# A depthwise convolution moved to tap matrices on TensorE, in a hybrid encoder layer

## The chip, the cores and the metric

The kernel runs on one core of a Trainium2 chip. The metric is the device time of one execution in microseconds (us). Names used: TensorE or PE (matrix products; "PEld" is its weight load), VectorE or DVE, ScalarE or ACT, GpSimd or POOL, SyncE or SP (it issues all the DMAs of this kernel). One execution is also recorded by the hardware profiler; durations of single instructions come from that one.

## What is computed

One encoder layer for 1024 tokens of width 1024, in float32. The part that matters here, shortened:

```python
p = h @ w_in + b_in                       # 3072 columns: conv value, conv gate, q, f, v, g (512 each)
u = p_value * sigmoid(p_gate)
y = depthwise_causal_conv(u, w_dw) + b_dw # 31 taps, 512 channels
cv = silu(group_norm(y) * gain + bias)    # 8 groups of 64 channels, per token
hg = hgrn2(q, f, v, g)                    # 4 heads of 128; gated linear recurrence over the tokens
y = concat(cv, hg) @ w_out                # then RMS norm, gate, residual
y2 = relu(h2 @ w_up) ** 2 @ w_down        # channel mixing, D_FF = 4096; then norm, gate, residual
```

## The kernel before

All engines' instructions are put in order when the kernel is built. `Weave` (line 168) is a small planner: it keeps a clock for each engine, charges each instruction an assumed cost (lines 251 to 254), and lets generators ("streams") run when their due time has come or their condition holds. The order found this way is the order in which each engine executes; on the chip an engine waits where an operand is late. SBUF is a pool of 53 slots of 128 x 1024 float32 (`Slots`); rings of slots hold loads (`stage`) and weights (`wring`).

Products of the main path are made of three matmuls of float32r (high part times high, high times low, low times high; `mm_k`, `mm_half`, `mm_step`), so every operand is split first into two slots (`split`: a copy by ACT, a subtraction by DVE or POOL). Matmuls of plain float32 operands run as two passes, and the trace counts two instructions for each of them.

The stages follow one another on PE:

- Start (to 76.7 us in the profiled execution): x is normalised and transposed, the modulation is computed, and three column blocks of `w_in` (`FIRST`) are multiplied as h arrives.
- Mixer (to 403.2 us): `mixer` (line 1076) goes through the column blocks of `w_in` in `ORDER`, 48 matmuls of 512 columns each (tiles `pj`). Weights are the stationary side, so a result has 128 channels as rows and all tokens as columns. v is the exception: `v_mm` (line 851) takes tokens as the stationary side, 256 columns at a time.
- Projection out (to 528.7 us): `out_mm` makes six token tiles from the blocks `EARLY` first, adds the blocks `LATE` later (tiles `pout`), and `out_tile` normalises, adds the residual and prepares h2.
- Up and down (to 1152.7 us): the feed-forward part in a two-level scheme of block products (tiles `pup`, `al`, `be`). The change does not touch its code.

Beside the projections, four blocks of the convolution run as streams. `conv_gate` and `conv_val` make u with channels as rows. `conv_near` (line 667) applies 20 taps by DVE, one scalar_tensor_tensor over up to 1024 tokens for each, into the PSUM tile `cacc`. `conv_far` (line 640) applies the other 11 taps in halves, with products by ACT or POOL and sums by POOL. `conv_norm` (line 685) transposes the result to tokens as rows (tile `cpt`), normalises in halves, and transposes back (tile `cpb`).

The four heads of the recurrence run as streams too. `head_att` (line 778) builds one score tile `att` for one head at a time. Blocks of h = 1, 2, 4, ... 64 tokens are joined level by level: PE computes the products of a level (tile `pl`), DVE multiplies the query, key and decay arrays for the next level, and for the levels in `MASKED` (1, 2, 4, 8) DVE copies the results under a mask. For h = 2, 4, 8 a level is one matmul with all 128 rows of a token tile as stationary side and 64 moving columns, for each of 8 token tiles; for h = 16, 32, 64 there is one matmul for each block of h. `head_state`, `head_out` and `put_mix` finish the head (tiles `tn`, `pS`, `po`, `pot`).

`mods_mid` loads further modulation weights (32 loads of `wada_n` in the whole kernel) and reduces them by DVE at a low rank. SP issues every load and store in one order.

## Time and profile before

| | us |
|---|---|
| median of 3 runs | 1161.85 (1156.34 to 1162.74) |
| profiled execution | 1161.52 |
| its span, first to last instruction | 1159.7 |
| mean granted TensorE clock in it | 0.971 of full |
| DMA traffic | 183.96 MB, 159 GB/s on average |

The table is read from the top: the profiled execution lies within the runs, so its durations can be set against the median. The granted clock is the share of full speed that the throttle allowed PE, averaged over the span.

### The profile page before, as it was taken

What the parts mean: (1) busy time and instruction counts of PE and PEld (TensorE: products, weight loads), DVE (VectorE), ACT (ScalarE), POOL (GpSimd) and SP (SyncE); (2) the same over time, 40 slices, a digit from 0 to 9 for tenths busy, and PEclk for the clock granted to TensorE, in tenths of its full rate; (3) what the DMA queues carried; (4) which work ended last, traced back from release to release, by engine and by line L of the source; (5) the groups of instructions that cost most, each with busy time, mean ns of one, the idle gap of its engine ahead of it and who ended that gap; (6) DMA issues with size and microseconds to landing.
All of it is one profiled execution on the core that took longest, in us unless ns stands there. A gap on an engine that the chain in (4) does not pass through costs nothing.

```text
span 1159.7 us, 14360 instructions
## 1 busy us (share of the span) xinstructions
PE 1090.5 (94%) x5606; PEld 909.5 (78%) x5606; DVE 845.0 (73%) x798; ACT 491.7 (42%) x691; POOL 479.6 (41%) x348
## 2 busy tenths in 40 slices
PE   3899879899998999978999999999999999999996
PEld 3787769787797788857888888888888888888885
DVE  5968988899999986464754986432356969996942
ACT  5643133323433353557544233566543434444520
POOL 6527778756688682484200232223400001304301
PEclk6899889989999999989999999999999999999999
DMA  9423213322311020355467774423666866674801
GB/s 371 165 65 109 74 54 110 127 80 85 92 37 37 26 85 1 117 210 200 145 256 276 293 263 164 135 76 133 220 254 228 319 225 231 246 262 158 323 22 73
DMA packets 50899, 183.96 MB, mean 159 GB/s; under 512 B 5648, under 2 KB 5904, under 8 KB 50832
## 3 DMA queue, kind: packets, MB, share of 16 engines
q1 hardware_dynamic: 50832, 183.05, 44.5%
q8 instruction: 44, 0.72, 0.3%
q14 instruction: 23, 0.19, 0.0%
HBM read 149.47 MB, written 33.55 MB: 158 GB/s over the span
## 4 chain that ended last, share of the span: by engine, by line
PE 54%; DVE 1%; POOL 0%; ACT 0%; DMA 0%; issue 0%; DVEq 0%; POOLq 0%; ACTq 0%
PE pup L1731 26%; PE al L1731 15%; PE be L1731 11%; PE pout L1731 1%; PE pt L1735 1%; DVE s L194 1%; POOL s L194 0%; ACT junk L194 0%; DMA x2d<-s 0%; PE pg L1731 0%; DVEq L1834 0%; POOLq L1834 0%; POOL last_ss L194 0%; POOL fr L194 0%; ACTq L1834 0%
## 5 line engine op out<-in xcount | busy, mean ns | idle before, releaser
L194 POOL TENSOR_TENSOR s<-s,s 128x1024 fp32r<-128x1024 f32 (+9 forms) x164 | 303.7, 1866 | 479.5 <-ACT s L194 443.6
L194 DVE TENSOR_TENSOR s<-s,s 128x1024 fp32r<-128x1024 f32 (+3 forms) x333 | 413.9, 1282 | 80.5 <-ACT s L194 56.1
L194 ACT ACTIVATE s<-s 128x1024 fp32r<-128x1024 f32 (+4 forms) x317 | 298.4, 972 | 298.9 <-DVE s L194 192.1
L1731 PE MATMUL pup<-s,s 128*128 128x512 f32 x1344 | 309.1, 391 | 0.0
L1731 PEld LDWEIGHTS pup<-s,s 128*128 128x128 f32 x1344 | 252.4, 188 | 52.1
L1731 PE MATMUL pj<-s,s 128*128 128x512 f32 (+1 forms) x1200 | 252.1, 366 | 0.0
L1731 PEld LDWEIGHTS pj<-s,s 128*128 128x128 f32 x1200 | 202.4, 193 | 33.0 <-ACT s L194 0.3
L1731 PE MATMUL al<-s,s 128*128 128x512 f32 x768 | 175.6, 390 | 3.1 <-DVE s L194 3.1
L1731 PEld LDWEIGHTS al<-s,s 128*128 128x128 f32 x768 | 143.9, 188 | 34.2 <-DVE s L194 4.3
L1731 PE MATMUL be<-s,s 128*128 128x512 f32 x576 | 131.0, 389 | 0.0
L1731 PEld LDWEIGHTS be<-s,s 128*128 128x128 f32 x576 | 108.1, 188 | 22.5
L1731 PE MATMUL pout<-s,s 128*128 128x512 f32 x384 | 96.4, 401 | 8.4 <-DVE s L194 8.3
L194 DVE SCALAR_TENSOR_TENSOR cacc<-s,vec,cacc 128x1023 f32<-128x1023 f32 (+18 forms) x76 | 96.9, 1275 | 1.1
L1731 PEld LDWEIGHTS pout<-s,s 128*128 128x128 f32 x384 | 71.1, 191 | 23.8 <-DVE s L194 9.2
L194 DVE SCALAR_TENSOR_TENSOR s<-s,c_act,s 128x1024 f32<-128x1024 f32 (+1 forms) x48 | 68.6, 1430 | 19.4 <-DMA s<-in_wada_n 18.0
L194 DVE SCALAR_TENSOR_TENSOR s<-pup,s 128x1024 f32<-128x1024 f32 x16 | 19.6, 1225 | 53.3 <-PE pup L1731 50.4
L194 DVE TENSOR_TENSOR s<-pup,s 128x1024 f32<-128x1024 f32 x24 | 29.3, 1222 | 40.0 <-PE pup L1731 40.0
L194 ACT ACTIVATE s<-s,vec 128x512 f32<-128x512 f32 (+5 forms) x40 | 28.3, 710 | 58.4 <-POOL s L194 58.3
L1731 PEld LDWEIGHTS pl<-s,s 128*16 128x16 f32 (+3 forms) x640 | 34.0, 137 | 21.9 <-issue 15.9
L1731 PE MATMUL pl<-s,s 128*16 128x16 f32 (+3 forms) x640 | 35.9, 222 | 14.8 <-DVE s L194 12.7
L1731 PE MATMUL pf<-s,s 128*128 128x512 f32 x144 | 41.3, 429 | 5.2 <-DVE s L194 3.7
L194 POOL TENSOR_SCALAR s<-s,vec 128x512 f32<-128x512 f32 (+6 forms) x44 | 45.3, 1031 | 0.0
(119 smaller groups left out, 757.1 us busy)
## 6 DMA issues: line engine op xcount, KB each, us to landing
s<-in_wdn SPq DMA_DIRECT2D x72, 512.0 KB, 5.2
s<-in_wup SPq DMA_DIRECT2D x56, 512.0 KB, 5.6
s<-in_wada_n SPq DMA_DIRECT2D x32, 512.0 KB, 3.5
s<-in_win SPq DMA_DIRECT2D x17, 512.0 KB, 3.6
s<-in_x SPq DMA_DIRECT2D x16, 512.0 KB, 6.4
s<-in_wada_t SPq DMA_DIRECT2D x16, 512.0 KB, 9.8
u<-s SPq DMA_DIRECT2D x16, 512.0 KB, 2.9
s<-u SPq DMA_DIRECT2D x16, 512.0 KB, 4.5
```

What stands on the lines that cost most here:

```text
L194: return op(*a, **k)
L1731: return self.te.matmul(out, lhsT=lhsT, rhs=rhs, **k)
L1735: return self.te.transpose(out, in_, identity)
```

## The change

The convolution becomes a product with matrices of taps. Value, gate and v are now computed with tokens as the stationary side (`t_mm`, four steps of 256 tokens each; the kinds `'U'`, `'G'` and `'V'` in `ORDER`), with their 512 columns as the moving side. u is written to a DRAM tensor `udram` in blocks of 32 tokens, one 512-byte piece for each token and quarter of the channels. `conv_input` loads it back in two passes of 256 channels: each partition takes one contiguous piece of 16 KiB, 63 token rows (31 of the block before and 32 of the block itself, a row of ones standing for the bias) twice over the two halves of the partitions. `conv_mm` multiplies each channel's 64 x 32 matrix of taps (loaded from the new input `toep`) with the 32 blocks as columns: 512 matmuls in plain float32. Their results come out with the tokens of a block as rows; ACT evacuates them, the normalisation runs over full tiles, and one transpose back remains (32 instead of 64 transposes for the convolution).

The levels h = 2, 4, 8 of the recurrence are issued as four matmuls of 32 stationary columns and 16 moving columns each, with results in four groups of 32 rows of PSUM; the masked copies become four of 32 rows. There are two score tiles, so a head may start while the one before it is unfinished. The planner's costs, the order of the column blocks, the early and late blocks, and ring sizes change with it. Four of the 53 slots become one wide tile while the convolution runs.

The core of the diff (imports of host arrays, slot bookkeeping and unchanged steps are left out):

```diff
-FIRST = (4, 0, 12)
-ORDER = (5, 8, 13, 9, 1, 6, 16, 2, 7, 14, 21, 10, 20, 3, 15, 18, 23, 11, 22)
+FIRST = (12, 8, 13)
+ORDER = (9, 20, 'V0', 'V1', 'V2', 'V3', 'G0', 'G1', 'G2', 'G3', 21, 'U0', 'U1', 'U2', 'U3', 14, 10, 22, 15, 11, 23)
-EARLY, LATE = (0, 4, 2, 5, 1, 6), (3, 7)
+EARLY, LATE = (4, 5, 0, 1, 2, 3), (6, 7)
-R0, STAGE, WRING = 12, 3, 6
+R0, STAGE, WRING, WRING1 = 12, 3, 12, 4
...
-    V = wv.engine(nc.vector, "V", lambda op, n: (0.13 if "scalar" in op else 0.07) + n / 960)
-    A = wv.engine(nc.scalar, "A", lambda op, n: 0.17 + n / 1190)
-    G = wv.engine(nc.gpsimd, "G", lambda op, n: 0.1 + n / (1000 if op == "tensor_scalar" else 460))
+    V = wv.engine(nc.vector, "V", lambda op, n: 0.16 + n / 930)
+    A = wv.engine(nc.scalar, "A", lambda op, n: 0.22 + n / 1190)
+    G = wv.engine(nc.gpsimd, "G", lambda op, n: 0.55 + n / (1350 if op == "tensor_scalar" else 520))
...
-    def conv_gate(j, ps):
-        yield room(1)
-        u = convs[j]["u"] = new()
-        A.activation(u.f, ps, AF.Sigmoid, bias=bcol(4 + j))
...
-    def conv_far(j):
...
-    def conv_near(j):
...
+    udram = dram.tile([4, CB, NB + 1, P], F32, name="udram")
+    crow_s = new()
+    S.dma_start(crow_s.f, crow.broadcast_to([P, 1024]))
+    sig = [None] * 4
+    ys = [None] * 4
+    u_rows = [0]
+
+    def t_gate(s, ps):
+        sig[s] = slots.new_last()
+        V.tensor_tensor(sig[s].f.rearrange("p (a c) -> p a c", c=512), ps.rearrange("p (a c) -> p a c", c=512),
+                        crow_s.f[:, None, H0].broadcast_to([P, 2, 512]), ALU.add)
+        A.activation(sig[s].f, sig[s].f, AF.Sigmoid)
+        yield
+
+    def t_val(s, ps):
+        yield room(1)
+        u = new()
+        V.tensor_tensor(u.f.rearrange("p (a c) -> p a c", c=512), ps.rearrange("p (a c) -> p a c", c=512),
+                        crow_s.f[:, None, H1].broadcast_to([P, 2, 512]), ALU.add)
+        mm.done(ps, "V")
+        G.tensor_tensor(u.f, u.f, sig[s].f, ALU.mult)
+        yield after("G")
+        for a in range(2):
+            for r in range(4):
+                b0 = 1 + 8 * s + 4 * a
+                nc.sync.dma_start(udram[r, :, b0:b0 + 4, :].rearrange("i q c -> q i c"),
+                                  u.f[:, (4 * a + r) * P:(4 * a + r + 1) * P])
+        wv.spend("S", 6.0)
+        u.release()
+        sig[s].release()
+        u_rows[0] += 1
+        if u_rows[0] == 4:
+            crow_s.release()
+            wv.add(conv_input(), RCONV)
+
+    def conv_input():
+        yield slots.gone
+        w = slots.wide().rearrange("p (b c) -> p b c", c=P)
+        for r in range(2):
+            S.dma_start(w[64 * r:64 * r + 1, 0, :], ones[0:1, :])
+            nc.sync.dma_start(w[64 * r:64 * r + 1, 1:, :], ones[1:CB, :])
+        for p in range(2):
+            yield room(4)
+            toeps = [new() for _ in range(4)]
+            for c in range(4):
+                S.dma_start(toeps[c].f, toep[p, c])
+            for r in range(2):
+                nc.sync.dma_start(w[64 * r + 1:64 * r + CB, :, :], udram[2 * p + r, 1:CB, 0:NB, :])
+                nc.sync.dma_start(w[64 * r + CB:64 * r + 64, :, :], udram[2 * p + r, :, 1:NB + 1, :])
+                wv.spend("S", 3.0)
+            yield wv.t["S"] + DLAT
+            yield from conv_mm(p, w, toeps)
+        slots.end_wide()
+
+    def conv_mm(p, w, toeps):
+
+        for q in range(2):
+            yield acc.free
+            ps = acc.take(ps_acc("cv"))
+            for i in range(16):
+                m = 16 * q + i
+                for c in range(4):
+                    for r in range(2):
+                        rows = slice(64 * r, 64 * r + 64)
+                        TE.matmul(ps[CB * c:CB * c + CB, 512 * r + CB * i:512 * r + CB * i + CB],
+                                  lhsT=toeps[c].f[rows, CB * m:CB * m + CB], rhs=w[rows, :, CB * c + m],
+                                  start=True, stop=True, us=0.03)
+            if q:
+                free(toeps)
+            wv.add(conv_evac(p, q, ps), 0)
+            yield
+
+    acc = Banks(wv, 1)
+
+    def conv_evac(p, q, ps):
+        pv = ps.rearrange("p (r i b) -> p r i b", r=2, i=16)
+        for s in range(4):
+            if ys[s] is None:
+                yield room(1)
+                ys[s] = new()
+            yv = ys[s].f.rearrange("t (b p r q i) -> t p q r i b", p=2, r=2, q=2, i=16)
+            for r in range(2):
+                A.activation(yv[:, p, q, r], pv[:, r, :, 8 * s:8 * s + 8], AF.Copy)
+        acc.done(ps, "A")
+        yield after("A")
+        if p and q:
+            for s in range(4):
+                wv.add(conv_norm(s), RNORM)
+
+    def conv_norm(s):
+
+        y = ys[s]
+        yield after("A")
+        yv = y.f.rearrange("p (a c) -> p a c", c=64)
+        mu = tiny("gmu", 16)
+        V.reduce_sum(mu, yv, axis=AX.X)
+        V.tensor_tensor(yv, yv, mu[:, :, None].broadcast_to([P, 16, 64]), ALU.subtract)
+        yield room(2)
+        sz, z = new(), new()
+        A.activation(sz.f, y.f, AF.Square)
+        var = tiny("gvar", 16)
+        V.reduce_sum(var, sz.f.rearrange("p (a c) -> p a c", c=64), axis=AX.X)
+        r = rstd_of(var, 16, 1.0 / 64, 1e-5, "gr")
+        V.tensor_tensor(yv, yv, r[:, :, None].broadcast_to([P, 16, 64]), ALU.mult)
+        for h in range(2):
+            yield aux_free
+            pb = ps1("cpb")
+            for b in range(4):
+                TE.transpose(pb[:, b * P:(b + 1) * P], y.f[:, (4 * h + b) * P:(4 * h + b + 1) * P], ident)
+            yield after("PE", 0.2)
+            pv = pb.rearrange("p (b c i) -> p c b i", c=4, i=CB)
+            zv = z.f[:, HALF[h]].rearrange("p (c b i) -> p c b i", c=4, i=CB)
+            for c in range(4):
+                A.activation(zv[:, c], pv[:, c], AF.Identity, bias=col(V_GNB + c), scale=col(V_GNG + c))
+            done1(pb, "A")
...
-    att_s = new()
-    att = att_s.f.rearrange("p (n t) -> p n t", t=P)
-    G.memset(att_s.f, 0.0)
+    att_s = [new(), new()]
+    atts = [t.f.rearrange("p (n t) -> p n t", t=P) for t in att_s]
+    for t in att_s:
+        G.memset(t.f, 0.0)
+    S.dma_start(udram[:, :, 0, :].rearrange("r i c -> (r i) c"), att_s[1].f[:, 0:P])
...
-        yield lambda: att_turn[0] == j
+        yield lambda: att_turn[0] >= j - 1
+        att = atts[j % 2]
...
-                    TE.matmul(pl[:, n * 64:(n + 1) * 64], lhsT=K[:, n * P:(n + 1) * P],
-                              rhs=Qn[:, n, :, 1, :], start=True, stop=True)
+                    for g in range(4):
+                        o = g * 32
+                        TE.matmul(pl[o:o + 32, n * 16:(n + 1) * 16], lhsT=K[:, n * P + o:n * P + o + 32],
+                                  rhs=Qn[:, n, g * nb // 4:(g + 1) * nb // 4, 1, :], start=True, stop=True, us=0.015)
...
-                V.copy_predicated(av[:, :, :, 1, :],
-                                  mk[:, None, :, :].broadcast_to([P, NT, nb, h]), plv)
+                if h == 1:
+                    V.copy_predicated(av[:, :, :, 1, :],
+                                      mk[:, None, :, :].broadcast_to([P, NT, nb, h]), plv)
+                else:
+                    plg = pl[:, 0:P].rearrange("p (n b i) -> p n b i", n=NT, i=h)
+                    for g in range(4):
+                        o, bs = g * 32, slice(g * nb // 4, (g + 1) * nb // 4)
+                        V.copy_predicated(av[o:o + 32, :, bs, 1, :],
+                                          mk[o:o + 32, None, bs, :].broadcast_to([32, NT, nb // 4, h]),
+                                          plg[o:o + 32])
...
-    def v_mm(j0):
...
+    def t_mm(kind, s):
+
+        if s == 0:
+            yield loads[0].has(4)
+            tws[:] = [loads[0].get() for _ in range(4)]
+        yield mm.free
+        ps = ps2("pt" + kind)
+        for k in range(KT):
+            w = tws[k // 2]
+            for q in range(2):
+                tsl = slice((2 * s % 4 + q) * P, (2 * s % 4 + q + 1) * P)
+                mm_half(TE, ps[:, HALF[q]], [t[:, tsl] for t in h_halves(k)[s // 2]],
+                        [t[:, HALF[k % 2]] for t in w], k == 0, k == KT - 1)
+            if s == 3 and k % 2:
+                if kind == [j for j in ORDER if isinstance(j, str) and j[0] in TGROUPS][-1][0]:
+                    wring.n = WRING1
+                loads[0].used()
+            yield
+        wv.add(dict(G=t_gate, U=t_val, V=v_evac)[kind](s, ps), 0)
+
+    tws = []
+
+    def v_evac(s, ps):
+        pv = ps.rearrange("p (n c) -> p n c", n=2)
+        if s == 0:
+            yield room(4)
+            for hd in heads:
+                hd["v"] = new()
+        yield lambda: "v" in heads[3]
+        for j, hd in enumerate(heads):
+            V.tensor_tensor(hd["v"].f[:, 256 * s:256 * s + 256].rearrange("p (n c) -> p n c", n=2),
+                            pv[:, :, j * P:(j + 1) * P],
+                            vbias[:, None, j * P:(j + 1) * P].broadcast_to([P, 2, P]), ALU.add)
+            hd["vh", s] = True
```

More of the change, by code (lines that the diff above doesn't have):

```diff
@@ L375, in x_load @@
     def x_load(n):
[L376 removed]
+        xn[n] = slots.new_last() if n < NWIDE else new()
         S.dma_start(xn[n].f, x[n * P:(n + 1) * P, :])
@@ L571, in rest @@
         for j in ORDER:
-            srcs += [winv[(j - 16) // 2, i] for i in range(2)] if 16 <= j < 20 else [win[j]]
+            if isinstance(j, int):
+                srcs.append(win[j])
+            elif j[1] == "0" and j[0] in TGROUPS:
+                srcs += [wint[TGROUPS.index(j[0]), i] for i in range(4)]
         loads.append(Loads(srcs, wring))
@@ L614, in put_mix @@
         yield from split(full, hi.r[:, sl], lo.r[:, sl])
-        marks.t["mix", kt, half] = wv.now
-    def tap(j, s):
-        return col(V_WDW + j * TAPS + PADW - s)
-    convs = [dict() for _ in range(4)]
+        for n in range(4):
+            marks.t["mix", kt, half * 4 + n] = wv.now
     heads = [dict() for _ in range(4)]
-    def conv_gate(j, ps):
-        yield room(1)
-        u = convs[j]["u"] = new()
-        A.activation(u.f, ps, AF.Sigmoid, bias=bcol(4 + j))
-        mm.done(ps, "A")
-        yield
@@ L665, in block_kernel @@
-    near_turn = [0]
-    def conv_near(j):
-        c = convs[j]
-        uf = c["u"].f
-        yield lambda: near_turn[0] == j
-        acc = ps_acc("cacc")
-        for s in range(0, TAPS - POOL_TAPS):
-            yield idle("V", NEAR)
-            if s == 0:
-                V.tensor_scalar(acc, uf, tap(j, 0), col(V_BDW + j), ALU.mult, ALU.add)
-            else:
-                V.scalar_tensor_tensor(acc[:, s:], uf[:, 0:T - s], tap(j, s), acc[:, s:], ALU.mult, ALU.add)
-        yield lambda: "far" in c
-        V.tensor_tensor(c["pacc"].f, acc, c["pacc"].f, ALU.add)
-        c["u"].release()
-        near_turn[0] += 1
-        for half in range(2):
-            wv.add(conv_norm(j, half), RNORM)
@@ L685, in conv_norm @@
-    def conv_norm(j, half):
-        y = convs[j]["pacc"]
-        yield after("V")
-        yield aux_free
-        pt = ps1("cpt")
-        for q in range(4):
-            n = half * 4 + q
-            TE.transpose(pt[:, q * P:(q + 1) * P], y.f[:, n * P:(n + 1) * P], ident)
-        yield after("PE", 0.2)
-        pv = pt.rearrange("p (a c) -> p a c", c=64)
-        mu = tiny("gmu", 8)
-        V.reduce_sum(mu, pv, axis=AX.X)
-        yield room(1)
-        scr = new()
-        yc, sq = scr.f[:, H0], scr.f[:, H1]
-        ycv = yc.rearrange("p (a c) -> p a c", c=64)
-        var = tiny("gvar", 8)
+        A.activation(sig[s].f, sig[s].f, AF.Sigmoid)
@@ L712, in conv_norm @@
         yield after("V")
-        yield aux_free
-        pb = ps1("cpb")
-        for q in range(4):
-            TE.transpose(pb[:, q * P:(q + 1) * P], yc[:, q * P:(q + 1) * P], ident)
-        yield after("PE", 0.2)
-        z, sz = yc, sq
-        A.activation(z, pb, AF.Identity, bias=col(V_GNB + j), scale=col(V_GNG + j))
-        done1(pb, "A")
-        A.activation(sz, z, AF.Sigmoid)
+        for h in range(2):
[9 more added lines that the diff above has]
+            done1(pb, "A")
@@ L722, in conv_norm @@
+        y.release()
+        A.activation(sz.f, z.f, AF.Sigmoid)
         yield after("A")
+        V.tensor_tensor(z.f, z.f, sz.f, ALU.mult)
+        sz.release()
+        yield after("V", 0)
         yield room(2)
-        yield from put_mix(j, half, lambda o: V.tensor_tensor(o, z, sz, ALU.mult))
-        scr.release()
-        if half:
-            y.release()
+        hi, lo = mix[s % 2, s // 2] = pair()
+        yield from split(z.f, hi.r, lo.r)
+        z.release()
+        for n in 2 * s, 2 * s + 1:
+            for k in range(4):
+                marks.t["mix", k, n] = wv.now
@@ L885, in head_state @@
     def head_state(j):
         hd = heads[j]
-        yield lambda: ("vh", 0) in hd and ("vh", 1) in hd
+        yield lambda: all(("vh", s) in hd for s in range(4))
         v, f = hd["v"].f, hd["f"].f
@@ L1008, in gate_rows @@
         acc.release()
-        grow[i] = new()
-        g = grow[i].f
+        gs = new()
+        g = gs.f
         yield ring.room()
@@ L1055, in mods_mid @@
     def mods_mid():
-        yield from gate_rows(0, stage)
         yield from ffn_cols(0, stage)
         yield from ffn_cols(1, stage)
+        yield from gate_rows(0, stage)
     for j, ps in zip(FIRST, pfirst):
@@ L1065, in load_wo @@
     def load_wo(k):
-        yield lambda: len(slots.free) >= WOSPARE + 2 and bool(stage.room()())
+        yield lambda: slots.left() >= WOSPARE + 2 and bool(stage.room()())
         hi, lo = pair()
@@ L1305, in stream @@
                 need = len(srcs) + extra
-                yield lambda: self.out < AHEAD and len(slots.free) >= need + RES
+                yield lambda: self.out < AHEAD and slots.left() >= need + RES
                 raws = []
```

205 lines of the change are left out of this document (96 added, 109 removed).

## Prediction

> **What bounds the kernel now.** I read the busy times first, then the slices by stage, then the chain that ended last, then the waits of the matmul engine in the one stage that is not full.
>
> ```profile
> span 1159.7 us, 14360 instructions
> PE 1090.5 (94%) x5606; PEld 909.5 (78%) x5606; DVE 845.0 (73%) x798; ACT 491.7 (42%) x691; POOL 479.6 (41%) x348
> PE 54%; DVE 1%; POOL 0%; ACT 0%; DMA 0%; issue 0%; DVEq 0%; POOLq 0%; ACTq 0%
> 0.00:23.50 23.50, 7.64 (x34) 6.86 (x34) 11.75 (x28) 14.12 (x28) 15.11 (x26) 0.67 0.93 362
> 23.50:76.70 53.20, 47.82 (x229) 38.27 (x229) 39.97 (x62) 29.41 (x54) 21.73 (x23) 0.89 0.45 167
> 76.70:403.20 326.50, 301.27 (x1925) 258.35 (x1925) 301.39 (x293) 105.70 (x188) 241.49 (x169) 0.96 0.23 73
> 403.20:528.70 125.50, 116.38 (x694) 96.44 (x692) 80.81 (x95) 66.09 (x132) 74.10 (x63) 0.97 0.33 116
> 528.70:844.30 315.60, 311.77 (x1387) 257.82 (x1386) 178.75 (x136) 153.74 (x156) 75.35 (x34) 0.99 0.54 192
> 844.30:1152.70 308.40, 305.27 (x1345) 251.78 (x1343) 230.18 (x184) 121.99 (x134) 50.91 (x32) 1.00 0.60 216
> ```
>
> The stage rows give start:end, length, busy time of PE, PEld, DVE, ACT and POOL, the granted clock, the DMA share and GB/s. The two feed-forward stages (528.7 on) are filled by PE at a clock of 0.99 to 1.00; the chain, followed back from the end, is PE through all of them. Nothing of the change lies there. The mixer (76.7 to 403.2) is different: PE and VectorE are both 92% busy (301.27 and 301.39 of 326.5 us) at a clock of 0.96. The projection out (to 528.7) has PE 93% busy at 0.97. I call these two the region: 452.0 us. Its PE waits:
>
> ```profile
> PE pl L1731 <- DVE s L194: 16.9, 12, 3.5
> PE pout L1731 <- DVE s L194: 8.3, 1, 8.3
> PE po L1731 <- DVE s L194: 2.9, 2, 2.7
> PE pot L1735 <- ACT s L194: 2.5, 2, 1.9
> PE pl L1731 <- DVE gsf L194: 2.0, 1, 2.0
> PE pg L1731 <- DVE s L194: 1.3, 1, 1.3
> ...
> PE pt L1735 <- POOL s L194: 3.8, 1, 3.8
> ```
>
> The last row lies behind 528.7 us and is used further down. The others are 33.9 us, 31.4 of them ended by VectorE. The lost clock adds 0.04 x 326.5 + 0.03 x 125.5 = 16.9 us (an estimate from the stage rows). So the region holds about 51 us in which PE waits or runs slowly, and the order of the instructions is fixed beforehand: PE cannot take later work while a level waits.
>
> **The change part by part, on PE.** Rates first: a 512-column matmul starts every 43.52/192 = 0.227 us; a 256-column one every (347.15 - 338.43)/72 = 0.121 us.
>
> ```profile
> 1018.75 43.52 PE al L1731 x192
> 338.43 8.88 PE L1731 MATMUL pj<-s,s 128*128 128x256 f32 x72
> 347.15 0.62 PE L1731 MATMUL pd<-s,ones_r 128*128 128x512 f32 x2
> ```
>
> *Projections.* Gate, value and v move from weights-stationary to tokens-stationary. Gate and value keep 2 x 192 matmuls of 512 columns; v goes from 384 of 256 to 192 of 512: 46.5 - 43.5 = **-3.0 us**.
>
> *Recurrence levels 2, 4, 8.* Before, each is 8 matmuls with 128 weight columns; the trace has two passes per float32 matmul:
>
> ```profile
> 125.48 1.89 PE L1731 MATMUL pl<-s,s 128*128 128x64 f32 x16
> 127.18 4.37 PE L1731 MATMUL pj<-s,s 128*128 128x512 f32 x18
> 147.57 0.71 PE L1731 MATMUL pl<-s,s 128*16 128x16 f32 x64 [2.87 <-DVE s L194]
> 148.20 5.77 PE L1731 MATMUL pj<-s,s 128*128 128x512 f32 x18
> 154.15 0.70 PE L1731 MATMUL pl<-s,s 128*32 128x32 f32 x32 [0.18 <-DVE s L194]
> 154.78 4.39 PE L1731 MATMUL pj<-s,s 128*128 128x512 f32 x18
> ```
>
> A level of the old form takes 127.18 - 125.48 = 1.70 us. The new form is 32 matmuls of 32 weight columns and 16 moving ones. The trace has 32 matmuls of 16 and 16 in 0.63 us, and 16 of 32 and 32 in 0.63 us (0.039 each). So the new level costs 0.63 to 32 x 0.039 = 1.26; I take 0.63, whose count and moving size are the same. 4 heads x 3 levels x (1.70 - 0.63) = **-12.8 us** (-5.3 at the other end).
>
> *Convolution.* 512 float32 matmuls of 64 rows, 32 weight columns and 32 moving columns (2 passes x 2 halves x 16 channels x 4 x 2), with moving elements 128 apart, in eight separate corners of the array. No row has that form. From below, 0.63/32 = 0.020 each, 10 us; from above 1.70/8 = 0.21 each, 109 us, if nothing overlaps. I take the nearest row, 32 and 32 columns: 512 x 0.039 = **+20.2 us**.
>
> The first of these rows bears on a rule of the Trainium skill: TensorE: Matmul & The Clock Gate, section "Wait — 56ns, not 53.3ns?", says that matmuls start no closer than about 25 ns however small they are. The trace does not agree: 64 passes in 0.63 us are one per 10 ns. By the page 1024 passes of the convolution would be 25.6 us and a level 1.6, an estimate, and the sum below 17 us higher.
>
> *Transposes.* 32 of the convolution's 64 go:
>
> ```profile
> 170.96 0.60 PE L1735 MATMUL cpt<-msk,s 128*128 128x128 f32 x4
> 171.31 0.96 PE L1731 MATMUL pj<-s,s 128*128 128x256 f32 x6
> ```
>
> 8 x 0.35 = **-2.8 us**.
>
> **VectorE and the waits.** What leaves VectorE:
>
> ```profile
> L194 DVE SCALAR_TENSOR_TENSOR cacc<-s,vec,cacc 128x1023 f32<-128x1023 f32 (+18 forms) x76 | 96.9, 1275 | 1.1
> L194 DVE TENSOR_SCALAR cacc<-s,vec 128x1024 f32<-128x1024 f32 x4 | 5.4, 1340 | 0.1
> L194 DVE TENSOR_TENSOR s<-cacc,s 128x1024 f32<-128x1024 f32 x4 | 4.9, 1224 | 3.6 <-POOL s L194 3.5
> L194 DVE TENSOR_TENSOR s<-pout,s 128x1024 f32<-128x1024 f32 x7 | 8.4, 1218 | 1.9 <-PE pout L1731 1.9
> L194 DVE SCALAR_TENSOR_TENSOR s<-s,s,pS 128x128 f32<-128x128 f32 x24 | 8.3, 347 | 0.7
> L194 DVE COPY_PREDICATED s<-msk,pl 128x512 f32<-128x512 uint32 x16 | 16.1, 1008 | 0.0
> ```
>
> The taps are 96.9 + 5.4 + 4.9 = 107.2 us. The new work, by the full-width row (1.22 us) and the 128-column one (0.35): 8 bias adds and some 24 full-width steps of the norm and splits, 39 us, of which about that much stood there before in halves; 16 v evacuations of 256 columns, about 0.5 each, 8 us; and 12 masked copies become 48 of 128 columns, 12 x (1.4 - 1.0) = 5 us. So about 95 of 382 us leave, and the share falls from 85% of the region to some 69% of a shorter one. POOL loses the far taps as well; ACT loses its tap products and gets 32 small evacuations (0.28 us for 128 columns), far below its 172 of 452 us.
>
> What do the waits become? At least nothing changes (0), at most all 51 us go. The nearest row is the up stage, VectorE 57% busy, with clock 0.99 and 3.8 us of PE idle: 2% of its length, 10 us in 452. The head chains (levels one after another) remain here, so I leave 15 us: **-36 us**. What is late next is the chain of levels itself and then the convolution's norm.
>
> **What is costed at nothing, and its cover.** The DRAM round trip: 2.1 MB out, 4.2 MB in, 4.2 MB of tap matrices, some 32 GB/s in a stage that moves 73. The 32 stores wait on SP for POOL's product; behind them stand weight loads, hence PE, and the cover is two projection blocks (48 x 0.227 = 10.9 us each). The convolution's matmuls are a new wait on PE for the block loads; behind them stand the projections of heads 2 and 3 and all levels still open, and ACT and VectorE wait for those. The norm must end before the second part of the early output tiles; its cover is 6 tiles x 6 x 6 x 0.227 = 49 us of out-projection. Without it some 20 us of norm would show. Head work starts earlier, and two score tiles let two heads overlap; that is in the 36.
>
> **Sum**, against the profiled execution's own 1161.5 us (span 1159.7 and 1.8 around it; the median of the runs is 1161.85): 1161.5 - 3.0 - 12.8 - 2.8 + 20.2 - 36 = **1127 us**. Its own range: waits -51 to -15, convolution 10 to 30 us: 1102 to 1158.
>
> **Rivals.**
>
> (1) *The block loads are late; slower than before.* Each of the two passes loads, for both row halves, 31 partitions of 16 KiB (508 kB) and 32 more. The first stage row shows what one of 16 DMA engines moves: 362/(16 x 0.93) = 24.3 kB/us. If a load of 31 pieces cannot be shared out, it takes 20.9 us, and two queue on the same engine: 41.8 us a pass. The plan in the code allows 3.0 us a load pair and 2.0 after it. Counting its 6.0 for the stores and 5.8 for the tap matrices, PE reaches the matmuls some 30 us early in each pass (stores 7 and loads 44 against 20; then 44 against 14) and waits 60 us in all. Other engines catch up meanwhile (-10), the cold clock costs 3: 1127 + 53 = **1180**, from 1145 to 1195. It decides from 17 us of wait a pass: there the gain of 34 is gone. For: 31 pieces cannot be shared evenly among 16 engines, and the plan prices this load like any other. Against: every load in the trace spreads evenly, 512 KB in 3.6 us, so the trace shows no such case.
>
> ```profile
> s<-in_win SPq DMA_DIRECT2D x17, 512.0 KB, 3.6
> ```
>
> The Trainium skill speaks for this rival: DMA: Bandwidth & Descriptors, section "Why a DMA increments its semaphore by 16 and not by 1", lets a transfer use the largest number of engines up to 16 that divides the slowest dimension of both sides, which for 31 is one. No run here shows it yet.
>
> (2) *The waits stay.* If they come from the levels' order and not from VectorE's load, only some 8 us go: **1155**. For: the level waits are short (16.9 us in 12). Against: no wait of PE before 403 us is ended by anything but a VectorE that is 92% busy, save 2.5 us.
>
> (3) *The small matmuls do not overlap*: 109 us for the convolution, **1216**. Against: 32 matmuls in 0.63 us.
>
> **How the numbers follow.** Forecast 0.45, rival 1 0.35, rival 2 0.13, rival 3 0.07. A change within 0.5% (5.8 us) is what a measurement of this kernel cannot tell from none. Faster: 0.45 + 0.2 x 0.35 + 0.5 x 0.13 = 0.58. Within: 0.15 x 0.35 + 0.4 x 0.13 = 0.11. Slower: the rest, 0.31. The range runs from the forecast's low end, 1102, through rival 1 to 1190; outside are rival 3 and the tails, under 0.2.
>
> **What would show it.** Each step has its place in the changed profile: a level of 2, 4 or 8 at 0.63 us; the convolution at 20 us of PE between first and last; VectorE below 75% in the mixer; PE waits on VectorE under 15 us. Rival 1 would show as one or two PE waits of about 30 us ended by the block loads, with DMA nearly idle; rival 2 as level waits of today's size. The forecast fails if the round trip is late or if the mixer's own chain, heads 2 and 3 at its end, becomes longer than the work that covers it.

## The result, and the profile after

The changed kernel takes 1236.71 us (median of 4 runs, 1235.92 to 1241.32) against 1160.07 us for the one before in the same job: ratio 1.0671, 95% interval 1.0629 to 1.0714. It is slower by about 77 us, on the side of rival 1 and beyond the upper end of the range.

The profiled execution (1237.09 us) by stage, as in the prediction: start:end, length, busy time of PE, PEld, DVE, ACT and POOL, granted clock, DMA share, GB/s. The second fence is the share line of its chain of waits.

```profile
span 1234.9 us, 17034 instructions
23.50:79.10 55.60, 49.09 (x228) 38.68 (x228) 39.28 (x60) 29.33 (x54) 24.35 (x25) 0.89 0.44 162
79.10:309.60 230.50, 223.79 (x1607) 183.80 (x1606) 119.34 (x170) 48.50 (x100) 41.19 (x22) 0.99 0.36 107
309.60:433.90 124.30, 40.84 (x1302) 33.35 (x1301) 19.98 (x28) 13.11 (x39) 3.76 (x2) 0.64 0.21 67
433.90:467.50 33.60, 29.65 (x223) 23.37 (x221) 31.65 (x40) 12.52 (x17) 15.26 (x7) 0.91 0.16 49
467.50:606.80 139.30, 123.16 (x865) 100.14 (x864) 88.48 (x106) 75.82 (x159) 64.82 (x51) 0.91 0.32 105
606.80:919.50 312.70, 310.61 (x1390) 256.77 (x1388) 178.75 (x135) 155.37 (x158) 78.81 (x36) 1.00 0.56 195
919.50:1227.90 308.40, 305.27 (x1344) 251.90 (x1343) 228.95 (x183) 121.81 (x134) 53.44 (x33) 1.00 0.62 216
```

```profile
PE 72%; DMA 9%; DVE 9%; issue 4%; POOL 2%; ACT 2%; another core or an unknown queue 2%; SPq 0%; DVEq 0%; POOLq 0%; ACTq 0%
```

Up and down are as they were (621.1 us against 624.0). The region, 452.0 us before, is now 79.1 to 606.8: 527.7 us, +75.7. The four rows of the region have PE busy for 223.79 + 40.84 + 29.65 + 123.16 = 417.4 us; before it was 301.27 + 116.38 = 417.7. **So PE's busy time came out the same; the whole loss is PE standing still**, 110.3 us where it was 34.3. The chain of waits has 9% DMA in it, where it had 0%. The second row (79.1 to 309.6 us) has PE 97% busy at a clock of 0.99, where the mixer before had 92% at 0.96; that fits VectorE's relief, but other things changed with it. The third row says where the time went: 124.3 us with PE 33% busy, the other engines 3 to 16%, and a DMA share of 0.21. PE's waits in the region (engine, tile, line, what ended them: total, times, longest), and the convolution's matmuls on PE in order of time:

```profile
PE cv L1833 <- DMA wide<-udram: 53.3, 3, 19.9
PE cv L1833 <- issue: 28.3, 6, 19.0
PE pout L1833 <- POOL s L234: 5.8, 1, 5.8
PE pout L1833 <- DVE s L234: 4.1, 1, 4.1
PE pl L1833 <- DVE s L234: 3.6, 4, 1.5
PE cpb L1837 <- ACT s L234: 3.5, 1, 3.5
```

```profile
328.61 0.28 PE L1833 MATMUL cv<-wide,s 64*32 64x32 f32 x2 [18.98 <-issue]
348.77 2.81 PE L1833 MATMUL cv<-wide,s 64*32 64x32 f32 x247 [19.87 <-DMA wide<-udram]
353.30 0.33 PE L1833 MATMUL cv<-wide,s 64*32 64x32 f32 x7 [1.73 <-issue]
...
394.21 0.28 PE L1833 MATMUL cv<-wide,s 64*32 64x32 f32 x2 [13.56 <-DMA wide<-udram]
414.33 2.69 PE L1833 MATMUL cv<-wide,s 64*32 64x32 f32 x236 [19.83 <-DMA wide<-udram]
```

Each pass stops twice: before its first matmul, and again after one matmul (two passes of the array, "x2"), which needs only the upper half of the partitions. Four waits, 72.2 us. The 18.98 us put down to "issue" are the same kind: the chain of waits has the loads there, issued on SP at these times:

```profile
296.57 0.35 SPq L722 DMA_DIRECT2D wide<-udram  x1
297.33 0.27 SPq L722 DMA_DIRECT2D wide<-udram  x1
364.98 0.24 SPq L722 DMA_DIRECT2D wide<-udram  x1
365.69 0.23 SPq L722 DMA_DIRECT2D wide<-udram  x1
```

```profile
296.57 30.62 DMA wide<-udram
365.97 48.22 DMA wide<-udram
```

The two loads of 31 rows (line 722) were issued 0.76 us apart, and the second released PE 348.77 - 328.61 = 20.2 us after the first, in the second pass 20.1 us. 508 kB in about 20 us is 25 kB/us, what one of the 16 DMA engines moved in the first stage row (24.3). While PE waits, the DMA share is 0.11, and through 19.8 us of the wait for the second load it is 0.06, about one engine of 16, at 26 GB/s:

```profile
309.60:353.60 44.00, 3.42 (x258) 3.12 (x257) 2.52 (x2) 1.06 (x1) 3.76 (x2) 0.53 0.11 39
328.90:348.70 19.80, 0.00 (x0) 0.00 (x0) 0.00 (x0) 0.00 (x0) 0.00 (x0) 0.50 0.06 26
```

The first load of each pair took longer: it landed 30.6 us after its issue in the first pass and released PE 29.2 us after it in the second. Tap matrices and loads of 32 rows were under way beside it; what share of the longer time is theirs isn't shown.

### The profile page after: what moved, and what is told of

It reads as the page before. It is cut to its first block, busy times and chain, and to the rows that moved or that the text cites. A ratio compares the mean times of both kernels' runs of the same rounds, so it can differ in the third digit from the quotient of the medians.

```text
span 1234.9 us, 17034 instructions
## 1 busy us (share of the span) xinstructions
PE 1091.9 (88%) x6988; PEld 896.1 (73%) x6988; DVE 721.3 (58%) x751; ACT 471.8 (38%) x687; POOL 298.1 (24%) x200
## 4 chain that ended last, share of the span: by engine, by line
PE 72%; DMA 9%; DVE 9%; issue 4%; POOL 2%; ACT 2%; another core or an unknown queue 2%; SPq 0%; DVEq 0%; POOLq 0%; ACTq 0%
PE pup L1833 24%; PE al L1833 14%; PE be L1833 11%; DVE s L234 7%; DMA wide<-udram 6%; PE pout L1833 6%; PE ptG L1833 3%; PE pj L1833 3%; PE ptV L1833 3%; POOL s L234 2%; PE ptU L1833 1%; PE pf L1833 1%; ACT s L234 1%; PE pl L1833 1%
## 5 line engine op out<-in xcount | busy, mean ns | idle before, releaser
L234 DVE TENSOR_TENSOR s<-s,s 128x1024 fp32r<-128x1024 f32 (+4 forms) x342 | 407.3, 1229 | 123.7 <-ACT s L234 73.9
L234 ACT ACTIVATE s<-s 128x1024 fp32r<-128x1024 f32 (+2 forms) x317 | 304.5, 993 | 330.0 <-DVE s L234 195.8
L234 POOL TENSOR_TENSOR s<-s,s 128x1024 fp32r<-128x1024 f32 (+3 forms) x87 | 198.5, 2290 | 595.0 <-ACT s L234 519.1
L234 DVE SCALAR_TENSOR_TENSOR s<-s,c_act,s 128x1024 f32<-128x1024 f32 (+1 forms) x48 | 58.0, 1208 | 105.2 <-DMA s<-in_wada_n 103.9
L1833 PE MATMUL pj<-s,s 128*128 128x512 f32 x432 | 109.3, 412 | 0.0
L1833 PEld LDWEIGHTS pj<-s,s 128*128 128x128 f32 x432 | 85.7, 200 | 19.0 <-ACT s L234 0.3
L1833 PE MATMUL cv<-wide,s 64*32 64x32 f32 x1024 | 13.1, 245 | 81.6 <-DMA wide<-udram 53.3
L1833 PEld LDWEIGHTS cv<-wide,s 64*32 64x32 f32 x1024 | 11.7, 124 | 84.2 <-issue 84.2
L1833 PE MATMUL ptV<-s,s 128*128 128x512 f32 x192 | 48.0, 398 | 0.0
L1833 PE MATMUL ptG<-s,s 128*128 128x512 f32 x192 | 45.8, 394 | 0.0
```

Source lines behind the costliest of these rows:

```text
L234: return op(*a, **k)
L1833: return self.te.matmul(out, lhsT=lhsT, rhs=rhs, **k)
```

## The experiments

Theory A is rival 1: each load of 31 rows runs on a single DMA engine, so the convolution's operands are late. Its rivals are that something else in those loads is slow (their 16 KiB pieces), that only the place of the matmuls in PE's order is wrong, or that the rest of the forecast failed too. Ratios are to the kernel before in the same job (1159 to 1160 us).

**1. The loads.** The first run issues the 31 rows as 16 and 15; the second keeps 31 rows and divides the pieces.

```diff
# e1
-nc.sync.dma_start(w[64 * r + 1:64 * r + CB, :, :], udram[2 * p + r, 1:CB, 0:NB, :])
+nc.sync.dma_start(w[64 * r + 1:64 * r + 17, :, :], udram[2 * p + r, 1:17, 0:NB, :])
+nc.sync.dma_start(w[64 * r + 17:64 * r + CB, :, :], udram[2 * p + r, 17:CB, 0:NB, :])
# e2
+for b in range(0, NB, 8):
+    nc.sync.dma_start(w[64 * r + 1:64 * r + CB, b:b + 8, :], udram[2 * p + r, 1:CB, b:b + 8, :])
```

> The changed kernel; each load of 31 rows is issued as one of 16 rows and one of 15, same order of everything else. Theory A (a load whose row count shares no divisor with 16 engines runs on one engine, 20 us each, two in a row per pass): the PE waits ended by the block loads fall from about 82 us to under 15, and the time from 1237 to 1140-1165. Theory B (pieces of 16 KiB, or 32 partitions written at once, are slow whatever the row count): no change, 1230-1245.

> The changed kernel; each load of 31 rows is issued as four loads of 31 rows with pieces of 4 KiB. Theory A: each still runs on one engine, so the waits stay at about 82 us and the time at 1230-1245. Theory B: the pieces are now those of the other loads of the kernel, so the waits fall under 30 us and the time under 1190.

With 16 and 15 rows: 1182.43 us, ratio 1.0206 (1.0177 to 1.0235). With 31 rows in pieces of 4 KiB: 1239.19 us, 1.0704 (1.0668 to 1.0741). The waits of the convolution's matmuls in e1, then the second waits of both passes in e2:

```profile
PE cv L1834 <- DMA wide<-udram: 11.7, 3, 6.2
PE cv L1834 <- issue: 11.3, 6, 3.1
```

```profile
353.65 2.79 PE L1834 MATMUL cv<-wide,s 64*32 64x32 f32 x246 [23.52 <-DMA wide<-udram]
421.16 2.65 PE L1834 MATMUL cv<-wide,s 64*32 64x32 f32 x234 [23.67 <-DMA wide<-udram]
```

The number of rows decides, not the size of the pieces: **54 of the 77 us are the 31-row loads.** More loads alone do not help: e2 has four for each of e1's two. The Trainium skill's rule (DMA: Bandwidth & Descriptors, section "Why a DMA increments its semaphore by 16 and not by 1") agrees: 31 has no divisor up to 16 but one. But e1 stayed 23 us above the kernel before; its expectation (1140 to 1165) was missed. The rest of the study is about these 23 us.

**2. Only the order.** The changed kernel with the planner's price for a pair of loads at 22 us.

```diff
-                wv.spend("S", 3.0)
+                wv.spend("S", 22.0)
```

> The changed kernel with its 31-row loads as they are; only the time that the planner reckons for a pair of them is raised from 3 to 22 us, so that TensorE's order puts the convolution's matmuls about 20 us later in each pass. Theory A, only the order was wrong (TensorE reached the matmuls before the rows were there): the 81.6 us waited at cv fall under 20 and the time falls to 1175 to 1195, as with the divided loads. Theory B, the loads' 40 us delay everything that hangs on the convolution, and TensorE runs out of other work: the waits leave cv and come back at the norm's transposes and the out-projection, and the time stays at 1215 to 1245.

1214.89 us, ratio 1.0475 (1.0459 to 1.0491): 22 us back, 0.1 us below theory B's band and far from A's. An honest price lets other work go first, but the waits at cv are still 46.8 us (20.0 on the loads, 22.8 put down to issue, 4.0 on ACT), which fits theory B: PE runs out of other work.

**3. The parts of the forecast, one at a time, in the kernel before.** The new levels alone; then the kernel without 19 of VectorE's 20 taps in each block of the convolution.

```diff
# e4: levels 2, 4, 8 in the kernel before
-TE.matmul(pl[:, n * 64:(n + 1) * 64], lhsT=K[:, n * P:(n + 1) * P], rhs=Qn[:, n, :, 1, :], ...)
+for g in range(4):
+    o = g * 32
+    TE.matmul(pl[o:o + 32, n * 16:(n + 1) * 16], lhsT=K[:, n * P + o:n * P + o + 32],
+              rhs=Qn[:, n, g * nb // 4:(g + 1) * nb // 4, 1, :], ...)
# e5: near taps
-for s in range(0, TAPS - POOL_TAPS):
+for s in range(0, 1):
```

> The kernel before, with only the levels 2, 4, 8 in column tiles and the masked copies in four parts; the order on every engine stays as it was. If PE's own time counts in the mixer (the prediction's step): 12 x 1.04 = 12 us less, 1145-1152. If the mixer runs at VectorE's pace: within 5 us of before, 1155-1165, with longer PE waits at the levels.

> The kernel before, without 19 of the 20 near taps of each block (they are left out of the result); this takes about 97 us off VectorE and nothing off PE. The prediction's step (VectorE's load makes the waits): PE waits and lost clock in mixer and out-projection fall from 51 to about 15 us, time 1120-1130. Rival (the waits come from the order of the levels): 1150-1160.

The levels alone: 1159.81 us, ratio 1.0008 (0.9993 to 1.0022). Their size is as predicted: on the changed kernel's PE

```profile
111.62 0.74 PE L1833 MATMUL pl<-s,s 128*32 128x16 f32 x64
112.28 1.65 PE L1833 MATMUL ptV<-s,s 128*128 128x512 f32 x6
```

a level starts 0.66 us before its successor (forecast 0.63). But in the kernel before with the new levels the time only turns into waits. Both rows are level waits; the second line number holds the new form:

```profile
PE pl L1743 <- DVE s L194: 15.8, 8, 3.5
PE pl L815 <- DVE s L194: 9.2, 4, 3.7
```

25.0 us in 12, where it was 16.9 in 12. PE's busy time in 76.7 to 529 us is 408.18 against 417.95 us, the length of the stretch the same.

VectorE relieved (300.4 us busy in 76.7 to 529 us, where it was 382.2): 1162.35 us, ratio 1.0037 (1.0020 to 1.0054), no gain at all. The windows of that run, with those of the kernel before below them:

```profile
76.70:300.00 223.30, 205.77 (x1313) 175.56 (x1312) 168.37 (x167) 77.97 (x147) 181.21 (x119) 0.98 0.28 94
403.00:430.00 27.00, 20.90 (x98) 17.91 (x97) 20.55 (x22) 5.68 (x7) 14.37 (x7) 0.79 0.18 58
```

```profile
76.70:300.00 223.30, 204.93 (x1257) 174.35 (x1256) 202.47 (x193) 69.16 (x129) 159.76 (x110) 0.94 0.27 86
403.00:430.00 27.00, 26.54 (x140) 21.46 (x138) 21.34 (x23) 17.73 (x40) 22.49 (x15) 1.00 0.31 98
```

The clock rises from 0.94 to 0.98 in the first 223 us, and the gain is gone at the join of projection and out-projection: PE busy 20.90 us of 27 at 0.79, where it had been 26.54 at 1.00. The first `pout` matmul starts at 393.25 us, where it stood at 403.24: 10 us were gained up to there and lost behind it.

This run shows less than its expectation claims, for two reasons. The taps left out are not charged to the planner, so PE's order changed as well: the last head's first product (`pd`) stands right behind the first six `pout` matmuls, at 394.62 us, where it was at 415.19. And POOL keeps its far taps (321.0 us busy in the region, 315.6 before), for which each block's norm still waits; beside them the levels' 56 VectorE steps took 1195 ns each, 1151 before, 726 in the changed kernel. So e5 shows that taking the near taps off VectorE gains nothing here; it does not show what the whole relief of the change is worth.

The old levels put back into e1, every group of instructions in the same order, give the same answer from the other side:

> The kernel with the 16 + 15 row loads (1182.43 us) with the recurrence levels of 2, 4 and 8 computed as before the change (8 matmuls of 128 x 64 columns and one masked copy each, in place of 32 of 32 columns and four masked copies), every group of instructions in the same order. Theory A, TensorE's work in the region counts on the path (as the convolution's matmuls did: 960 left out gave 23.6 us): 12 levels x 1.07 us = 12.8 us come back, 1190 to 1197. Theory B, a level's matmuls lie in the wait for the level's own chain (masked copy and scaling on VectorE) or the shorter level only lengthens the next wait, as in the kernel before, where the same edit gave 0: 1179 to 1186.

1182.31 us against 1182.43: theory B. In neither kernel are the levels worth anything on the path that these runs can tell from nothing (e3 and e1 are known to some 3 us each); 12.8 us is ruled out.

**4. What the convolution's matmuls cost.** e1 with 15 of every 16 steps left out (480 of the 512 matmuls; the 960 of the expectation counts their two passes each).

```diff
+                        if i:
+                            TE.spend(0.03)
+                            continue
                         TE.matmul(ps[CB * c:CB * c + CB, 512 * r + CB * i:512 * r + CB * i + CB], ...
```

> The kernel with the 16 + 15 row loads, leaving out 15 of every 16 steps of the convolution's matmuls (960 of 1024; the planner still reckons their time, so every other instruction keeps its place; a memset of the bank on VectorE stands in, and the output isn't the reference's). Theory A, TensorE's own work in the passes bounds: its 960 matmuls at 16.4 ns (15.7 us) and the 11.3 us of issue waits between them go, 1182.4 falls to 1153 to 1160. Theory B, the chain of loads, copies, norm and transposes into the out-projection bounds: the matmuls' time comes back as waits, 1172 to 1183.

1158.82 us, ratio 0.9999 (0.9981 to 1.0018): theory A, 23.6 us less. The expectation's 16.4 ns a pass came from a wrong count of a burst: by the timeline row of the changed kernel above, 247 passes take 2.81 us, 11.4 ns each, so 960 make 10.9 us. The gaps put down to issue fell from 11.3 us in e1 to 1.8 in e9; the two together are 20.4 of the 23.6 us. With no tap left on any engine and hardly a matmul in their place, the changed kernel is only level with the one before.

**5. The bursts.** Handing the matmuls out 32 at a time, with a k step of the projection after each: the edit of e10 is shown; e6 had a bare `yield` in the last line.

```diff
                                   start=True, stop=True, us=0.03)
+                if i % 4 == 3:
+                    yield wv.now + 0.05
```

> The kernel with the 16 + 15 row loads (1182.43 us), and the convolution's matmuls handed out 32 at a time (four of the 16 steps of a bank), so that one k step of the projection (six 128x512 matmuls) stands between two handfuls, where it had 128 in a row. Theory A, the bursts starve the instruction stream: the 11.3 us of PE's waits at cv put down to issue (6 waits, 1.0 to 2.4 us each, one about every 128 matmuls) fall under 3, the granted clock of 310 to 405 us rises, and the time falls by 8 to 15 us, to 1167 to 1174. Theory B, what is late is the chain of the convolution's results into the out-projection: the issue waits may go, but the same time is waited ahead of the out-projection, 1178 to 1186.

> The kernel with the 16 + 15 row loads, the convolution's matmuls handed out 32 at a time with one k step of the projection (six 128x512 matmuls) after each 32; the earlier attempt left handfuls of 64 to 128 in a row. Theory A, the gaps put down to issue come from long bursts of matmuls of 10 to 16 ns: they fall from 11.3 us to under 3 and the time to 1166 to 1174. Theory B, the gaps come with the matmuls' number, however they are spread (PE's time per 32 stays near 0.75 us, 24 ns each): 1176 to 1184.

e6: 1178.94 us, ratio 1.0152 (1.0124 to 1.0181), inside the band of theory B. Its edit did less than the expectation says: a stream that yields without a due time is run again at once, and handfuls of up to 128 stayed. Its waits aren't read. e10, with all handfuls at 32: 1172.89 us, 1.0105 (1.0080 to 1.0130), theory A:

```profile
PE cv L1836 <- DMA wide<-udram: 9.8, 2, 4.9
PE cv L1836 <- issue: 2.8, 1, 2.8
```

11.3 us of issue waits became 2.8, and the time fell by 9.5 us. (The second pass also came later in PE's order, so the two can't be told apart fully.)

The length of a burst is not what makes the stops, though. In e1 two of them stand 128 passes apart:

```profile
330.91 1.31 PE L1834 MATMUL cv<-wide,s 64*32 64x32 f32 x108
333.19 1.51 PE L1834 MATMUL cv<-wide,s 64*32 64x32 f32 x128 [0.98 <-issue]
336.65 0.43 PE L1834 MATMUL cv<-wide,s 64*32 64x32 f32 x20 [1.94 <-issue]
```

Counted in the trace from the kernel's first matmul, the seven stops of e1 put down to issue come after 2123, 2250, 2378, 2632, 2760, 3015 and 3143 passes, the last one ahead of a level's matmul. Those of e10 come after 2505 and 2759, those of e11 (below) after 1994, 2758 and 3268. All lie within 3 passes of one grid with a step of 127.5, whatever the order of the work and the length of the bursts. So the stops go with the count of PE's instructions (the trace has one weight load for each pass). Small matmuls reach the next mark within 1.5 us; in e10, with wide matmuls between, most marks show no stop. What PE waits for at a mark isn't shown.

**6. The norm in one heap.** e10 still loses at the join. Its windows:

```profile
310.00:400.00 90.00, 73.30 (x1570) 57.31 (x1568) 51.55 (x74) 27.67 (x72) 19.64 (x10) 0.92 0.51 124
400.00:430.00 30.00, 13.48 (x124) 10.00 (x128) 26.88 (x27) 14.09 (x26) 22.88 (x10) 0.62 0.28 88
430.00:480.00 50.00, 46.31 (x446) 38.67 (x439) 24.84 (x45) 28.78 (x68) 5.82 (x4) 0.89 0.11 33
```

In 400 to 430 us PE is busy 13.48 of 30 us, VectorE 26.88 and POOL 22.88. Every token block holds all channels, so no block can be normalised before the last pass; before, each channel block's norm began when its own taps were done. e13 is e10 without the norm's arithmetic, its price still reckoned so that PE's order stays.

```diff
-        mu = tiny("gmu", 16)
-        V.reduce_sum(mu, yv, axis=AX.X)
...
-        V.tensor_tensor(yv, yv, r[:, :, None].broadcast_to([P, 16, 64]), ALU.mult)
+        wv.spend("V", 1.26)
```

> The kernel of e10 (16 + 15 row loads, convolution in handfuls of 32, 1172.9 us), leaving out the arithmetic of the convolution's norm (mean, variance, inverse root and the two scalings of four token blocks; copies, transposes and gate stay; the planner still reckons the time, so every group of TensorE's instructions keeps its place, and the output isn't the reference's). Theory A, the norm of four blocks in one heap after the last pass is where the relief is given back: the stretch of 400 to 430 us (TensorE 13.5 of 30 us busy, clock 0.62) fills, and the time falls by 10 to 18 us, to 1155 to 1163, at the kernel before (1159). Theory B, the heads' own chain and POOL's differences of the split (7 in a row, 18.4 us, in the run with 16 + 15 rows) hold that stretch: 1167 to 1174.

1159.58 us, ratio 1.0001 (0.9988 to 1.0015): 13 us less, theory A. Its window of the same stretch, and of the next:

```profile
400.00:430.00 30.00, 18.91 (x322) 15.19 (x323) 23.84 (x37) 15.42 (x28) 8.31 (x4) 0.77 0.21 71
430.00:480.00 50.00, 50.00 (x298) 41.98 (x297) 15.73 (x27) 24.66 (x60) 3.31 (x3) 1.00 0.09 33
```

Better, not full: other work at the join (VectorE 23.84 of 30 us) remains. The run prices the norm's arithmetic at 13 us; that its lying in one heap is what costs is not shown by it, and e14 below speaks against it.

**7. Attempts to make it pay.** The projection's column blocks in another order, so that the convolution starts earlier (e8, e11, e12), and the norm's statistics taken by pass (e14 to e16). What each moved:

```diff
-ORDER = (9, 20, 'V0', ..., 'G0', ..., 'G3', 21, 'U0', ..., 'U3', 14, ...)
+ORDER = (9, 'V0', ..., 'G0', ..., 'U0', ..., 'U3', 20, 21, 14, ...)      # e8, e11, e16
+ORDER = ('V0', ..., 'G0', ..., 'U0', ..., 'U3', 9, 20, 21, 14, ...)      # e12
+ORDER = (9, 20, 'V0', ..., 'G0', ..., 'U0', ..., 'U3', 21, 14, ...)      # e15
...
-        if p and q:
-            for s in range(4):
-                wv.add(conv_norm(s), RNORM)
+        if q:                                                            # e14, e15, e16
+            for s in range(4):
+                wv.add(conv_stats(s, p), RNORM)
```

> The 16 + 15 row loads, the convolution's matmuls 32 at a time, the planner's figure for a pair of loads at 8 us where it was 3, and the two projection blocks 20 and 21 moved behind the U blocks, so that two blocks of some 29 us of TensorE each lie between the last U block and the end of the projection. Theory A, what is left of the loss is that too little other work lies beside the convolution's loads and its norm: waits of the mixer and out-projection fall from 42 us to under 20 and the granted clock rises, 1140 to 1158 us, at or under the kernel before (1159.0). Theory B, the waits only move (the gates of heads 0 and 1 become late, slots are held longer): 1170 to 1190.

> The kernel with blocks 20 and 21 behind the U blocks (1169.66 us), with the convolution's matmuls 32 at a time and a k step of the projection between. Theory A, long bursts cost: the 12.1 us of issue waits at cv fall under 4 and the time to 1156 to 1164, at the kernel before (1159.0). Theory B, the cost goes with the number of matmuls: 1166 to 1174.

> As the run with blocks 20 and 21 behind the U blocks and the handfuls of 32 apart, and block 9 (the key of a head) moved behind the U blocks as well, so that the convolution's input is complete another 29 us of TensorE earlier. If cover for the loads and the norm is still short, the waits at cv for the rows and at the out-projection fall once more, 1150 to 1162; if the heads' levels, which start later, are now what is late, 1166 to 1185.

> The kernel of e10 with the norm's statistics and scaling taken for the 64-channel groups of each pass as soon as that pass is copied out of the bank (eight groups of each block after the first pass, eight after the second), where all sixteen waited for the second. Theory A: half of the norm's work leaves the heap, -5 to -9 us, 1164 to 1168. Theory B: 1169 to 1176.

> As the run with the norm by pass, with block 21 (a head's gate) moved behind the U blocks, so that the convolution's passes begin some 29 us of TensorE earlier relative to the end of the projection. Theory A (the heap is what costs, and cover for it helps): 1154 to 1164. Theory B: 1168 to 1178.

> As the run before, with block 20 behind the U blocks too and the planner's figure for a pair of loads at 5 us. Theory A: 1152 to 1162, at or under the kernel before. Theory B, the heads of blocks 20 and 21 become late: 1168 to 1180.

| run | us | ratio (95% interval) |
|---|---|---|
| e8, blocks 20 and 21 later | 1169.66 | 1.0092 (1.0075 to 1.0108) |
| e11, the same with handfuls of 32 | 1177.17 | 1.0148 (1.0125 to 1.0171) |
| e12, block 9 later too | 1171.23 | 1.0106 (1.0089 to 1.0123) |
| e14, e10 with the norm by pass | 1173.03 | 1.0115 (1.0098 to 1.0133) |
| e15, e14 with block 21 later | 1173.54 | 1.0126 (1.0099 to 1.0153) |
| e16, blocks 20 and 21 later, loads priced at 5 us | 1182.24 | 1.0201 (1.0183 to 1.0219) |

e8 gained 12.8 us on e1, but its edit had three parts (order, the price of the loads, the bare `yield` of e6) and stayed above the expected 1158. e11 missed both of its bands: the issue waits fell from 12.1 to 5.9 us, not under 4, and its first 128 matmuls still came in one burst; waits for POOL and ACT grew (pd <- ACT 6.1, pout <- POOL 7.0), and it is 7.5 us slower than e8. So the benefit of small handfuls in e10 is not a rule. e12, e14 and e15 lie in the bands of their second theories, e16 above both of its. The expectations count a column block at some 29 us of PE; the first matmul of the convolution moved by less, 15.9 us for block 21 (319.1 to 303.2, e14 to e15) and 20.9 us for block 9 (296.7 to 275.8, e11 to e12). In e14 half of the norm moved earlier and nothing was gained: in 400 to 430 us PE is busy 14.50 us and VectorE 28.07. No version found here beats the kernel before.

## Why the prediction was wrong, step by step

- **The choice of the likeliest case failed first.** The forecast took the round trip through DRAM to be covered; rival 1 gave the opposite with its mechanism, and that is what happened: loads on one engine, PE waiting, DMA nearly idle. "Every load in the trace spreads evenly" was the argument against it, and it was no evidence: every load quoted for it had 128 rows. Rival 1's "20.9 us" was right for the second load of a pair (20.1 to 20.2 measured). Its "60 us" of waits was too small: 72.2 us in the four waits and 81.6 us with the gaps inside the bursts, because the two loads of a pass took 52.2 and 49.4 us from the first issue to the second release, where it had 44. The "-10" for engines that catch up did not appear; they stood nearly still as well. Undoing it gave 54 us, its "+53"; as two of its parts were off, that the sums agree is luck. Its 1180 is too low because it starts from the forecast's 1127: with the loads mended the kernel takes 1182, 55 us more.
- **"-36", the waits that VectorE's relief would take away, was wrong.** The reading was that 31.4 of 33.9 us of PE's waits were ended by VectorE, hence that its load made them. In the kernel before, without the near taps, what was gained up to the out-projection was lost behind it (e5, with the limits said there). In the changed kernel the relief came and was larger than forecast: VectorE is busy 256.4 us of the region in e1, where it was 382.2 before and some 287 were expected. The level waits did go there: 16.9 us before, 3.6 after, 1.7 in e1 (15.0 again in e10). Other waits took their place, so that with the loads mended PE's idle time in the region grows instead of falling, 471.3 - 419.2 = 52.1 us against 34.3. The sum of e1's windows over the region, 80.9 to 552.2 us, and some of its waits there:

```profile
sum 471.30, PE 419.24 PEld 341.96 DVE 256.40 ACT 150.12 POOL 126.86; mean PE 83.85 PEld 68.39 DVE 51.28 ACT 30.02 POOL 25.37
```

```profile
PE pout L1834 <- POOL s L234: 5.8, 1, 5.8
PE pout L1834 <- DVE s L234: 4.2, 1, 4.2
PE cpb L1838 <- ACT s L234: 3.5, 1, 3.5
PE pl L1834 <- DVE s L234: 1.7, 2, 1.5
```

  Of the 52.1 us, 23.0 are waits of the convolution's own matmuls; the other 29.1, against 33.9 listed before, lie mostly at the join with the out-projection. So the step that failed is the one from "VectorE ended the wait" to "without its load the time is gained". That was rival 2's outcome, though not its reason: the level waits went, and the time did not.
- **"-12.8", the levels:** the size was right (0.66 us against 0.63), the place wrong. They lie in waits; on the path they are worth nothing that e4 and e3 can tell from zero.
- **"+20.2", the convolution's matmuls:** near in the sum (23.6 us for 480 of 512, e9), not in its parts. A matmul takes 0.023 us where "0.039" was forecast, and gaps of 1 to 3 us in the bursts, which no row of before showed, make up most of the rest. That two errors nearly cancel is luck. Rival 3 (109 us) is refuted.
- **"-3.0" and "-2.8", v and the transposes:** not tried alone on the path. PE's busy time by tile, in which pipelined matmuls overlap, fell by 3.4 us for the projections (252.1 to 248.7) and by 3.0 us for the convolution's transposes (9.6 to 6.6): near the forecast. That PE's busy time in all, 417.7 and 417.4 us, also fits the sum of the four terms (-3.0 - 12.8 - 2.8 + 20.2 = +1.6) is partly chance, since the convolution's matmuls were busy for 13.1 us.
- **"its cover is 6 tiles x 6 x 6 x 0.227 = 49 us", the norm:** this was mis-sized. `EARLY` is now (4, 5, 0, 1, 2, 3), and 0 to 3 are the convolution's own blocks, so the out-projection asks for the norm's result after the blocks 4 and 5 of the first two tiles: 24 matmuls, 5.4 us at 0.227. The "some 20 us" that would show without cover were 13 us (e13).
- **Two sums are off by a rounding:** the lost clock is 16.8 us, not 16.9, and the chance of "within" comes to 0.10, not 0.11. Nothing hangs on either.

In sum: 1160 + 54 (loads, e1) + 23.6 (conv matmuls, e9) = 1238, against 1236.7 measured. The two terms are steps down from the changed kernel, e1 and then e9, so that the sum closes says one thing only: e9, with the new projections, the levels, the relief and the norm in it, is level with the kernel before, and all these together are worth about 0. How they divide isn't shown, and e13's 13 us may overlap with the 23.6. Still open: what PE waits for at the stops put down to issue, which of the chains at the join is the last, and what the relief would be worth in a better order.

## What to carry to other kernels

Before a load replaces arithmetic, count the rows of its slowest dimension: 31 rows took as long as one DMA engine needs for all of them, and 16 + 15 rows gave back 54 us. A wait that ends with a busy engine isn't yet time to be gained: relieve that engine in the kernel before, as in e5 but with the order of the instructions held, before the relief is booked. When work moves from a stream that finishes piece by piece to passes that finish together, go through what the next stage asks for first, and count the cover only up to there: here 24 matmuls, not 216.

## What the runs showed of the hardware that was not expected

- A burst of 64-row, 32-column float32 matmuls ran at 11.4 ns a pass (247 passes in 2.81 us) and the column-tiled levels at 10 ns (64 in 0.66 us). The 25 ns in the Trainium skill (TensorE: Matmul & The Clock Gate, section "Wait — 56ns, not 53.3ns?") isn't a floor for either.
- In such bursts PE stops for 1 to 3 us at a time with nothing awaited that the trace shows. The stops stand on a grid of 127.5 passes, counted from the kernel's start, in e1, e10 and e11 alike; with wider matmuls between (e10) most marks show none (2.8 us of stops at cv, 11.3 in e1).
- VectorE was faster per instruction where POOL did less: the same 56 instructions took 1151 ns each before and 726 ns after, POOL being busy 315.6 and 125.0 us of the region. In e5, with VectorE's own load down by 82 us and POOL's as before (321.0 us), they took 1195 ns. The first row is of the kernel before, the second of the one after:

```profile
L194 DVE TENSOR_TENSOR s<-s,s 128x512 f32<-128x512 f32 x56 | 62.2, 1151 | 4.6 <-PE pl L1731 4.6
```

```profile
L234 DVE TENSOR_TENSOR s<-s,s 128x512 f32<-128x512 f32 x56 | 38.4, 726 | 29.5 <-PE pl L1833 29.4
```
